# The merge of two branches: both halves in the same form, all their ways through DRAM on SyncE's queue

## The chip, the core and the metric

The kernel runs on one core of a Trainium2 chip. The metric is the time of one execution in microseconds (us) of device time, as the median of several runs. The profile is a hardware trace of one execution. Its engines are TensorE (PE; PEld is its weight load), VectorE (DVE), ScalarE (ACT), GpSimd (POOL) and SyncE (SP), which here only issues DMAs.

## The reference, cut to what matters

One decoder layer over 256 tokens of 1024 features, in float32: a feed-forward block, a mixing sub-layer with two branches, a second feed-forward block and a final norm. The change lies at the end of the mixing sub-layer:

```python
y_attn = attn @ w_branch_attn[l]       # (256, 512) @ (512, 1024)
y_gmlp = gm @ w_branch_gmlp[l]         # (256, 512) @ (512, 1024)
gates = jax.nn.sigmoid(n @ w_gate[l] + b_gate[l])
merged = gates[..., :D] * y_attn + gates[..., D:] * y_gmlp
h = h + merged @ w_out[l]
h = h + 0.5 * swiglu(rmsnorm(h, ffn2_norm[l]), ffn2_w_gate[l], ffn2_w_up[l], ffn2_w_down[l])
```

## The kernel before, in words

**Precision.** Every float32 operand of a product is split into a high and a low part (`split`, L192): ACT casts the source to the high part (L193), DVE subtracts it to get the low part (L195). A product is then three matmuls, high by high, high by low and low by high (`mm3`, L186 to L190). The output projection works the other way around, with weights stationary (`by_passes`, L169): per block of 128 input features one matmul of 512 columns (L162) takes high and low activations side by side, and one of 256 (L167) the low weights.

**Weights.** They come in units of two half units of 512 KB. `fetch_to` (L129) issues the fetches on SyncE (L137) into seven raw buffers, `split_half` (L139) splits them into a ring of four split units, and `unit(i, ahead)` (L154) hands out unit i after splitting up to i + ahead: 3 ahead for `ALONE`, 2 for `PAIRED`. A raw buffer is free again when its half unit has been subtracted on DVE, a place in the ring when the matmuls of the unit four earlier are done. The four units of the branch products are numbered from `mb` (gMLP, attention, gMLP, attention; 512 output columns each), then come four of the projection (`mo`) and those of the second feed-forward (`f2`).

**Order.** TensorE and SyncE run in the order in which the program is written. In this part DVE and ACT do so too (`in_order`, L208). A DMA issue on ACT therefore stands in line with ACT's casts, and a fetch on SyncE in line with the other transfers there.

**The merge (L704 to L763).** Tokens are in partitions: for token halves j = 0, 1 the branch products come in PSUM, DVE multiplies by the gates (in `gates`, the attention's in the first 1024 columns, the gMLP's in the second), adds the two, and transposes 32 x 32 squares (L720). The projection needs features in partitions. The squares are put in place by a **way** through DRAM: a write-out to `m_way` (`leave`, L723) and four fetch-backs into `m_back`, one for each 32 partitions (`from_way`, L358 to L363). `settle` (L725) then splits what came back, 128 features at a time, into `mT` (in the profile `mg`).

The 1024 columns go in three pieces: 0 to 255, 256 to 511 and 512 to 1023. In the first two, the gMLP's and the attention's products for one token half share one PSUM bank and one multiplication (L743) gates both. The write-out is on ACT's queue, the fetch-backs on SyncE's. In the third, the products are 512 columns wide, each with its own multiplication (L754); after each branch one of the first two pieces is settled (L758). Its write-out goes per token half on ACT, and its eight fetch-backs (L760) are on ACT too.

The projection (`down_features`, L252, called at L767) has eight accumulators in the eight PSUM banks (a pool in which banks are taken in turn) and goes through the four units: unit 0 and 1 need piece 0 and piece 1, units 2 and 3 the third. Unit 0 is computed for six accumulators first, then for the last two. `unit` is called at the head of each; `behind` runs after the first and the second unit, and there `third` (L762) settles the third piece. After the last unit come the residual, the norm's high and low parts, and the second feed-forward (L768 on).

Of the kernel before, what the change touches and what calls it, by code (L numbers as in the profile page):

```python
# [18 lines left out]
P = 128  # L19
# [26 lines left out]
def block_kernel(ctx, tc, t, out):  # L46
# [107 lines left out]
    def unit(i, ahead=PAIRED):  # L154
        split_to(i + 1 + ahead)
        return parts[i]
# [29 lines left out]
    def mm3(ps, st, mv_, first, last):  # L186
        (sh, sl), (mh, ml) = st, mv_
        nc.tensor.matmul(ps, sh, mh, start=first, stop=False)  # L188
        nc.tensor.matmul(ps, sh, ml, start=False, stop=False)  # L189
        nc.tensor.matmul(ps, sl, mh, start=False, stop=last)  # L190
# [164 lines left out]
                    mm3(ps[j], st, (w[:, k, 0, :], w[:, k, 1, :]), u + k == 0, u == 1 and k == 3)  # L355
        return ps

    def from_way(to, way, queue=nc.sync, js=slice(NT)):  # L358

        squares32 = way.rearrange("(q r) a n -> r q a n", r=32)  # L360
        qs = slice(4 * js.start if js.start else 0, 4 * js.stop)
        for a in range(4):
            queue.dma_start(to[32 * a:32 * a + 32, qs], squares32[:, qs, a, :])  # L363

    def by_token(way):
        return way.rearrange("(j p) a n -> p j (a n)", p=P)
# [6 lines left out]
    class Hidden:  # L373
# [22 lines left out]
        def leave(self, c):  # L396
            p, e = divmod(c, 2)
            n = 32 * self.blocks(p)
            if e == 0:
                self.way[p] = dram.tile([S, 4, n], F32, name=f"{self.name}way{p}")  # L400
            nc.sync.dma_start(by_token(self.way[p])[:, :, CH * e:CH * (e + 1)], self.turned.pop(c))
# [110 lines left out]
    with in_order():  # L512
# [178 lines left out]
        for j in range(NT):  # L691
# [9 lines left out]
        gate(3, chunk(mg, nT2, "g", 3))  # L701


        pieces = ((0, 256), (256, 256), (512, 512))  # L704
        m_way = [dram.tile([S, 4, n // 4], F32, name=f"mway{c0}") for c0, n in pieces]
        m_turned = [tmp.tile([P, NT, n], F32, tag="hg", name=f"mt{c0}") for c0, n in pieces[:2]] + [ut]
        m_back = [mix_b[:, b:b + n // S * 2].rearrange("p a (q n) -> p (a q) n", n=n // 4)
                  for b, (c0, n) in zip((8, 10, 12), pieces)]

        def branch(ps, i, of, j, c0, n):  # L710
            w, c = unit(mb + i, ALONE if i != 1 else PAIRED), c0 % 512
            for k in range(4):
                st = tuple(p[:, j * P:(j + 1) * P] for p in block_of([of], k))
                mm3(ps, st, tuple(w[:, k, two, c:c + n] for two in range(2)), k == 0, k == 3)

        def merged(p, j):
            c0, n = pieces[p]
            m = gates[:, j, c0:c0 + n]
            nc.vector.tensor_add(m, m, gates[:, j, D + c0:D + c0 + n])
            nc.vector.transpose(m_turned[p][:, j], m)  # L720

        def leave(p, js=slice(NT)):
            nc.scalar.dma_start(by_token(m_way[p])[:, js], m_turned[p][:, js])  # L723

        def settle(p):  # L725
            c0, n = pieces[p]
            for b in range(n // P):
                k = c0 // P + b
                settle_in(mT[k // 4][:, k % 4:k % 4 + 1], m_back[p][:, :, b * 32:(b + 1) * 32])

        aoT, = alloc_T("ao", ("nC",))
        for hp in range(4):
            attend(hp)
        both = ((1, gmT), (0, aoT))
        for p in range(2):
            c0, n = pieces[p]
            pbs = [bank(f"pb{p}{j}") for j in range(NT)]
            for q, j in [(q, j) for q in range(2) for j in range(NT)] if p == 0 else [(q, j) for j in range(NT) for q in range(2)]:
                at, of = both[q]
                branch(pbs[j][:, at * n:(at + 1) * n], q, of, j, c0, n)  # L740
                if q:
                    m = gates[:, j].rearrange("p (q c) -> p q c", q=2)[:, :, c0:c0 + n]
                    nc.vector.tensor_mul(m, pbs[j].rearrange("p (q c) -> p q c", q=2), m)  # L743
                    merged(p, j)
            leave(p)
            from_way(m_back[p], m_way[p])
        mT = alloc_T("mg", ("nA", "nB"))
        c0, n = pieces[2]
        for q, (at, of) in enumerate(both):
            for j in range(NT):  # L750
                ps = bank(f"pb2{q}{j}")
                branch(ps, 2 + q, of, j, c0, n)
                m = gates[:, j, at * D + c0:at * D + c0 + n]
                nc.vector.tensor_mul(m, ps, m)  # L754
                if q:
                    merged(2, j)
                    leave(2, slice(j, j + 1))
            settle(q)  # L758
        for j in range(NT):
            from_way(m_back[2], m_way[2], nc.scalar, slice(j, j + 1))  # L760

        def third():  # L762
            settle(2)  # L763


        nT3 = alloc_T("n3", ("nC", "nD"))
        down_features(mo, 4, lambda k: both_of(mT, k), 1.0, gain3, nT3, "3", "aT", 1, [lambda: None, third])  # L767
        hidden = Hidden("f2")  # L768
        sums = [chunk(f2, nT3, "f2", 0), chunk(f2, nT3, "f2", 1, [0])]
        rs = token_factors("3")  # L770
# [70 lines left out]
def _packed(inputs):  # L841
# [12 lines left out]
    def columns(g, n):  # L854
# [8 lines left out]
             for n in (1, 2)}  # L863
# [5 lines left out]


    four = np.arange(512).reshape(4, 4, P // 4).transpose(1, 0, 2).reshape(-1)
    merged = np.concatenate([c0 + np.arange(256).reshape(4, 2, P // 4).transpose(1, 0, 2).reshape(-1)
                             for c0 in (0, 256)] + [512 + four])

    def chunks(w):
        return w.reshape(2, 4, P, -1, 512).transpose(3, 0, 2, 1, 4).reshape(-1, P, 4, 512)
# [38 lines left out]
```

## Time and profile before

| | |
|---|---|
| median of 3 runs | 534.79 us (534.17 to 535.75) |
| profiled execution, its own time | 533.75 us |
| its span in the trace | 532.0 us |
| mean granted clock of TensorE | 0.993 |
| busy: PE, PEld, DVE, ACT | 518.8, 435.2, 356.9, 264.5 us |
| DMA | 124.72 MB, 234 GB/s on average |

Instructions are named by the line that issued them, often a helper's; `out<-in` gives the tiles written and read. A releaser is what ended an engine's idle time. Stretches are in microseconds from the start of the span. A granted clock of 1.00 is 2.4 GHz, and 1.2 GHz is half of it; a mean between them mixes both.

### The profile page before, as it was taken

What the parts mean: (1) busy time and instruction counts of PE and PEld (TensorE: products, weight loads), DVE (VectorE), ACT (ScalarE), POOL (GpSimd) and SP (SyncE); (2) the same over time, 40 slices, a digit from 0 to 9 for tenths busy, and PEclk for the clock granted to TensorE, in tenths of its full rate; (3) what the DMA queues carried; (4) which work ended last, traced back from release to release, by engine and by line L of the source; (5) the groups of instructions that cost most, each with busy time, mean ns of one, the idle gap of its engine ahead of it and who ended that gap; (6) DMA issues with size and microseconds to landing.
All of it is one profiled execution on the core that took longest, in us unless ns stands there. A gap on an engine that the chain in (4) does not pass through costs nothing.

```text
span 532.0 us, 6846 instructions
## 1 busy us (share of the span) xinstructions
PE 518.8 (98%) x2490; PEld 435.2 (82%) x2490; DVE 356.9 (67%) x493; ACT 264.5 (50%) x366; POOL 12.2 (2%) x20
## 2 busy tenths in 40 slices
PE   9999999999999999999999996999999999999995
PEld 7888888888888888888888985888888888888884
DVE  6886676665454689489876683789764765575424
ACT  7754454544354466659555243467443544463402
POOL 0010000000000001000000000001000000000002
PEclk9999999999999999999999999899999999999998
DMA  8999597979677239977899375629798779677302
GB/s 320 368 338 308 163 340 257 273 206 279 187 199 282 80 123 337 346 217 205 247 326 356 124 205 170 235 80 321 238 250 297 229 276 334 177 240 230 137 0 79
DMA packets 60657, 124.72 MB, mean 234 GB/s; under 512 B 9424, under 2 KB 34000, under 8 KB 60496
## 3 DMA queue, kind: packets, MB, share of 16 engines
q1 hardware_dynamic: 58352, 122.39, 71.5%
q10 hardware_dynamic: 2272, 1.90, 1.1%
q8 instruction: 19, 0.31, 0.2%
q14 instruction: 14, 0.11, 0.1%
HBM read 112.21 MB, written 12.06 MB: 234 GB/s over the span
## 4 chain that ended last, share of the span: by engine, by line
PE 84%; DMA 6%; DVE 4%; issue 2%; ACT 1%; SPq 0%; ACTq 0%; POOLq 0%; DVEq 0%; POOL 0%
PE f L188 14%; PE f L189 14%; PE f L190 14%; PE acc L162 9%; PE acc L167 5%; PE acch L190 4%; PE acch L188 4%; PE acch L189 4%; PE g L190 3%; PE g L189 3%; PE g L188 3%; DVE w L195 2%; DMA qk<-qkway 2%; DMA qback<-qkway 1%; DMA qkway<-mixed 1%
## 5 line engine op out<-in xcount | busy, mean ns | idle before, releaser
L195 DVE TENSOR_TENSOR w<-raw,w 128x1024 fp32r<-128x1024 f32 x180 | 211.7, 1217 | 84.4 <-ACT w L193 84.1
L193 ACT CAST w<-raw 128x1024 fp32r<-128x1024 f32 x180 | 179.6, 1048 | 104.3 <-PE f L190 47.3
L190 PE MATMUL f<-w,n 128*128 128x512 f32 x336 | 130.7, 389 | 0.0
L188 PE MATMUL f<-w,n 128*128 128x512 f32 x336 | 130.7, 389 | 0.0
L189 PE MATMUL f<-w,n 128*128 128x512 f32 x336 | 130.7, 389 | 0.0
L190 PEld LDWEIGHTS f<-w,n 128*128 128x128 f32 x336 | 63.1, 188 | 13.2
L188 PEld LDWEIGHTS f<-w,n 128*128 128x128 f32 x336 | 63.1, 188 | 13.1
L189 PEld LDWEIGHTS f<-w,n 128*128 128x128 f32 x336 | 63.1, 188 | 13.0
L162 PE MATMUL acc<-f1h,w 128*128 128x512 f32 x176 | 43.4, 391 | 0.0
L162 PEld LDWEIGHTS acc<-f1h,w 128*128 128x128 f32 x176 | 31.9, 188 | 5.8
L188 PE MATMUL acch<-w,f2h 128*128 128x512 f32 x84 | 32.7, 389 | 0.0
L190 PE MATMUL acch<-w,f2h 128*128 128x512 f32 x84 | 32.7, 389 | 0.0
L189 PE MATMUL acch<-w,f2h 128*128 128x512 f32 x84 | 32.7, 389 | 0.0
L388 ACT ACTIVATE f2s<-f,rstd 128x256 f32<-128x256 f32 x22 | 10.3, 474 | 30.2 <-PE f L190 28.9
L188 PE MATMUL g<-w,n 128*128 128x512 f32 x64 | 24.9, 389 | 0.0
L189 PE MATMUL g<-w,n 128*128 128x512 f32 x64 | 24.9, 389 | 0.0
L190 PE MATMUL g<-w,n 128*128 128x512 f32 x64 | 24.9, 389 | 0.0
L167 PEld LDWEIGHTS acc<-f1h,w 128*128 128x128 f32 x176 | 23.5, 191 | 1.5
L162 PE MATMUL acc<-mg,w 128*128 128x512 f32 x64 | 18.6, 424 | 5.6 <-DVE mg L195 5.6
L167 PE MATMUL acc<-f1h,w 128*128 128x256 f32 x176 | 23.9, 282 | 0.0
L390 DVE SCALAR_TENSOR_TENSOR f2a<-f,rstd,f2s 128x256 f32<-128x256 f32 x22 | 10.5, 476 | 19.4 <-ACT f2s L388 19.4
L388 ACT ACTIVATE f1s<-f,rstd 128x256 f32<-128x256 f32 x22 | 10.3, 473 | 24.3 <-PE f L190 22.8
(173 smaller groups left out, 623.7 us busy)
## 6 DMA issues: line engine op xcount, KB each, us to landing
raw<-in_f SPq DMA_DIRECT2D x84, 512.0 KB, 6.5
raw<-in_f1d SPq DMA_DIRECT2D x22, 512.0 KB, 6.2
raw<-in_f2d SPq DMA_DIRECT2D x22, 512.0 KB, 6.0
raw<-in_gate SPq DMA_DIRECT2D x16, 512.0 KB, 6.9
raw<-in_out SPq DMA_DIRECT2D x8, 512.0 KB, 5.6
f1way<-f1t SPq DMA_DIRECT2D x11, 256.0 KB, 6.4
f2way<-f2t SPq DMA_DIRECT2D x11, 256.0 KB, 5.5
front<-in_first SPq DMA_DIRECT2D x7, 384.0 KB, 5.8
```

The lines of the kernel that those rows point to most:

```text
L162: nc.tensor.matmul(ps, st, both.rearrange("p two n -> p (two n)"), start=first, stop=last)
L167: nc.tensor.matmul(ps[:, n:], st, both[:, 0, :], start=False, stop=False)
L188: nc.tensor.matmul(ps, sh, mh, start=first, stop=False)
L189: nc.tensor.matmul(ps, sh, ml, start=False, stop=False)
L190: nc.tensor.matmul(ps, sl, mh, start=False, stop=last)
L193: nc.scalar.copy(hi, src)
L195: nc.vector.tensor_sub(lo, src, hi.bitcast(F32))
L388: nc.scalar.activation(sg, ps[j][:, :CH], AF.Silu, scale=rs[j])
L390: nc.vector.scalar_tensor_tensor(a, ps[j][:, CH:], rs[j], sg, op0=ALU.mult, op1=ALU.mult)
```

## The change

Both halves of the 1024 columns are handled by one function, `merge(hf)`. First the gMLP's products of 512 columns are computed and gated for both token halves, then the attention's in two quarters of 256 columns. Each quarter is multiplied, added, transposed and written out at once, and after both write-outs of a half come its eight fetch-backs. All write-outs and fetch-backs are on SyncE's queue, and ACT issues none. In the second half a quarter of the first is settled after each gMLP product. The attention's unit of the first half is asked for with `ALONE`, that of the second with `PAIRED`, so that one unit of projection weights is split at each `unit` call of the merge except the last, and the third unit of the projection at the head of its first. `behind` settles quarter 2 after the projection's first unit and quarter 3 after its second. On the host, the order of the projection's input features follows the quarters. The other calls of `from_way` do the same as before.

```diff
-    def from_way(to, way, queue=nc.sync, js=slice(NT)):
+    def from_way(to, way):
...
-            queue.dma_start(to[32 * a:32 * a + 32, qs], squares32[:, qs, a, :])
+            nc.sync.dma_start(to[32 * a:32 * a + 32], squares32[:, :, a, :])
...
-        pieces = ((0, 256), (256, 256), (512, 512))
-        m_way = [dram.tile([S, 4, n // 4], F32, name=f"mway{c0}") for c0, n in pieces]
...
+        m_way = [dram.tile([S, 4, UC // 4], F32, name=f"mway{p}") for p in range(4)]
+        m_turned = {}
+        m_back = [mix_b[:, b:b + 2].rearrange("p a (q n) -> p (a q) n", n=UC // 4) for b in (8, 10, 12, 14)]
...
+        def merge(hf):
+            w = unit(mb + 2 * hf, ALONE)
+            for j in range(NT):
+                ps = bank(f"pg{hf}{j}")
+                branch(ps, w, gmT, j, slice(512))
+                m = gates[:, j, D + 512 * hf:D + 512 * (hf + 1)]
+                nc.vector.tensor_mul(m, ps, m)
+                if hf:
+                    settle(j)
+            w = unit(mb + 2 * hf + 1, PAIRED if hf else ALONE)
+            for p in (2 * hf, 2 * hf + 1):
+                m_turned[p] = tmp.tile([P, NT, UC], F32, tag="hg", name=f"mt{p}")
+                for j in range(NT):
+                    ps = bank(f"pa{p}{j}")[:, :UC]
+                    branch(ps, w, aoT, j, slice((p % 2) * UC, (p % 2 + 1) * UC))
+                    m = gates[:, j, p * UC:(p + 1) * UC]
+                    nc.vector.tensor_mul(m, ps, m)
+                    nc.vector.tensor_add(m, m, gates[:, j, D + p * UC:D + (p + 1) * UC])
+                    nc.vector.transpose(m_turned[p][:, j], m)
+                nc.sync.dma_start(by_token(m_way[p]), m_turned[p])
+            for p in (2 * hf, 2 * hf + 1):
+                from_way(m_back[p], m_way[p])
...
-        for p in range(2):
...
-                    nc.vector.tensor_mul(m, pbs[j].rearrange("p (q c) -> p q c", q=2), m)
-                    merged(p, j)
-            leave(p)
-            from_way(m_back[p], m_way[p])
+        merge(0)
         mT = alloc_T("mg", ("nA", "nB"))
...
-                if q:
-                    merged(2, j)
-                    leave(2, slice(j, j + 1))
-            settle(q)
-        for j in range(NT):
-            from_way(m_back[2], m_way[2], nc.scalar, slice(j, j + 1))
...
+        merge(1)
...
-        down_features(mo, 4, lambda k: both_of(mT, k), 1.0, gain3, nT3, "3", "aT", 1, [lambda: None, third])
+        down_features(mo, 4, lambda k: both_of(mT, k), 1.0, gain3, nT3, "3", "aT", 1,
+                      [lambda: settle(2), lambda: settle(3)])
```

## Rows read from the trace of the kernel before

**Rows 1.** TensorE's waits, whole execution: line, what it waited for, us in all, times, longest.

```profile
PE acc L162 <- DVE mg L195: 5.6, 2, 4.5
```

**Rows 2.** The table by stretches: length, busy us (x instructions) of each engine, granted clock, DMA.

```profile
293.32:304.94 11.62, 11.62 (x99) 11.62 (x98) 8.14 (x15) 2.48 (x5) 0.00 (x0) 1.00 0.35 122
304.94:315.84 10.90, 10.90 (x50) 9.01 (x49) 9.03 (x12) 6.41 (x8) 0.00 (x0) 1.00 0.59 145
315.84:332.94 17.10, 11.52 (x66) 9.84 (x64) 8.80 (x14) 4.54 (x9) 0.00 (x0) 1.00 0.62 206
332.94:340.19 7.25, 7.25 (x33) 6.16 (x33) 5.49 (x7) 3.17 (x4) 0.00 (x0) 0.76 0.86 280
340.19:345.78 5.59, 5.59 (x35) 4.88 (x33) 4.54 (x12) 2.65 (x6) 0.00 (x0) 1.00 0.47 185
345.78:525.00 179.22, 179.22 (x801) 148.76 (x800) 114.08 (x156) 83.28 (x104) 3.96 (x5) 1.00 0.65 209
```

**Rows 3.** Timeline of TensorE: start, us, instruction, in brackets the idle time before it.

```profile
315.84 2.88 PE L162 MATMUL acc<-mg,w 128*128 128x512 f32 x12
...
322.67 3.90 PE L162 MATMUL acc<-mg,w 128*128 128x512 f32 x16 [1.11 <-DVE mg L195]
...
332.94 5.50 PE L162 MATMUL acc<-mg,w 128*128 128x512 f32 x16 [4.46 <-DVE mg L195]
```

**Rows 4.** Timeline of ACT, the same stretch (ACTq: a DMA issue).

```profile
319.25 2.39 ACTq L723 DMA_DIRECT2D mway<-mixed  x2
321.75 0.71 ACT L193 CAST mg<-mixed 128x256 fp32r<-128x256 f32 x2 [8.05 <-DMA raw<-in_f]
322.46 6.55 ACTq L363 DMA_DIRECT2D mixed<-mway  x8
329.11 1.99 ACT L193 CAST w<-raw 128x1024 fp32r<-128x1024 f32 x2 [6.65 <-DMA mixed<-mway]
331.01 1.32 ACT L193 CAST mg<-mixed 128x256 fp32r<-128x256 f32 x4
```

**Rows 5.** Timeline of DVE, the same stretch.

```profile
322.19 0.76 DVE L195 TENSOR_TENSOR mg<-mixed,mg 128x256 fp32r<-128x256 f32 x2 [0.93 <-ACT mg L193]
330.19 2.36 DVE L195 TENSOR_TENSOR w<-raw,w 128x1024 fp32r<-128x1024 f32 x2 [7.24 <-ACT w L193]
332.46 1.43 DVE L195 TENSOR_TENSOR mg<-mixed,mg 128x256 fp32r<-128x256 f32 x4
```

**Rows 6.** Groups of DVE's instructions from 290 to 346, by form: busy us, mean ns.

```profile
L754 DVE TENSOR_TENSOR mixed<-pb,mixed 128x512 f32<-128x512 f32 x4 | 2.6, 674 | 0.0
L720 DVE STREAM_TRANSPOSE mt<-mixed 128x256 f32<-128x256 f32 x4 | 1.8, 445 | 0.1
...
L195 DVE TENSOR_TENSOR ao<-po,ao 128x256 fp32r<-128x256 f32 x4 | 1.4, 418 | 1.0 <-ACT ao L193 1.0
```

**Rows 7.** DMA issues, whole execution: transfer, queue, count, KB each, median us to landing.

```profile
raw<-in_f SPq DMA_DIRECT2D x84, 512.0 KB, 6.5
...
gmback<-gmway SPq DMA_DIRECT2D x4, 128.0 KB, 10.4
mway<-mt ACTq DMA_DIRECT2D x2, 256.0 KB, 2.8
mixed<-mway SPq DMA_DIRECT2D x8, 64.0 KB, 2.1
...
mixed<-mway ACTq DMA_DIRECT2D x8, 64.0 KB, 4.5
```

**Rows 8.** The way's DMA issues: ns min/median/max of one issue, first and last start.

```profile
L363 SPq DMA_DIRECT2D mixed<-mway x8: 302/445/612, 304.5 to 310.6; - x8
```

**Rows 9.** SyncE's own waits from 311 to 324.

```profile
SPq L137 <- DMA mway<-mixed: 6.1, 1, 6.1
```

**Rows 10.** DMA queue of SyncE from 304.5 to 306.9: packets, MB, share of 16 engines.

```profile
q1 hardware_dynamic: 730, 0.18, 32.1%
```

**Rows 11.** DMA queue of ACT from 322 to 330, the same columns.

```profile
q10 hardware_dynamic: 1276, 0.78, 36.0%
```

More of the change, by code (lines that the diff above doesn't have):

```diff
@@ L356, in chunk @@
         return ps
-    def from_way(to, way, queue=nc.sync, js=slice(NT)):
+    def from_way(to, way):
         squares32 = way.rearrange("(q r) a n -> r q a n", r=32)
-        qs = slice(4 * js.start if js.start else 0, 4 * js.stop)
         for a in range(4):
-            queue.dma_start(to[32 * a:32 * a + 32, qs], squares32[:, qs, a, :])
+            nc.sync.dma_start(to[32 * a:32 * a + 32], squares32[:, :, a, :])
     def by_token(way):
@@ L701, in block_kernel @@
         gate(3, chunk(mg, nT2, "g", 3))
-        pieces = ((0, 256), (256, 256), (512, 512))
-        m_way = [dram.tile([S, 4, n // 4], F32, name=f"mway{c0}") for c0, n in pieces]
[L706 to L711, printed above, removed]
+        m_way = [dram.tile([S, 4, UC // 4], F32, name=f"mway{p}") for p in range(4)]
@@ L712, in branch @@
+        m_turned = {}
+        m_back = [mix_b[:, b:b + 2].rearrange("p a (q n) -> p (a q) n", n=UC // 4) for b in (8, 10, 12, 14)]
+        def branch(ps, w, of, j, c):
             for k in range(4):
                 st = tuple(p[:, j * P:(j + 1) * P] for p in block_of([of], k))
[L714 to L720, printed above, removed]
@@ L722, in leave @@
-        def leave(p, js=slice(NT)):
-            nc.scalar.dma_start(by_token(m_way[p])[:, js], m_turned[p][:, js])
+                mm3(ps, st, tuple(w[:, k, two, c] for two in range(2)), k == 0, k == 3)
         def settle(p):
-            c0, n = pieces[p]
-            for b in range(n // P):
-                k = c0 // P + b
+            for b in range(2):
+                k = 2 * p + b
                 settle_in(mT[k // 4][:, k % 4:k % 4 + 1], m_back[p][:, :, b * 32:(b + 1) * 32])
+        def merge(hf):
[20 more added lines that the diff above has]
+                from_way(m_back[p], m_way[p])
@@ L733, in block_kernel @@
             attend(hp)
-        both = ((1, gmT), (0, aoT))
-        for p in range(2):
[L736 to L740, printed above, removed]
-                if q:
-                    m = gates[:, j].rearrange("p (q c) -> p q c", q=2)[:, :, c0:c0 + n]
-                    nc.vector.tensor_mul(m, pbs[j].rearrange("p (q c) -> p q c", q=2), m)
-                    merged(p, j)
-            leave(p)
-            from_way(m_back[p], m_way[p])
-        mT = alloc_T("mg", ("nA", "nB"))
-        c0, n = pieces[2]
-        for q, (at, of) in enumerate(both):
-            for j in range(NT):
[L751 to L755, printed above, removed]
-                    merged(2, j)
-                    leave(2, slice(j, j + 1))
-            settle(q)
-        for j in range(NT):
-            from_way(m_back[2], m_way[2], nc.scalar, slice(j, j + 1))
-        def third():
-            settle(2)
+        merge(0)
+        mT = alloc_T("mg", ("nA", "nB"))
+        merge(1)
         nT3 = alloc_T("n3", ("nC", "nD"))
-        down_features(mo, 4, lambda k: both_of(mT, k), 1.0, gain3, nT3, "3", "aT", 1, [lambda: None, third])
+        down_features(mo, 4, lambda k: both_of(mT, k), 1.0, gain3, nT3, "3", "aT", 1,
+                      [lambda: settle(2), lambda: settle(3)])
         hidden = Hidden("f2")
@@ L871, in _packed @@
     four = np.arange(512).reshape(4, 4, P // 4).transpose(1, 0, 2).reshape(-1)
-    merged = np.concatenate([c0 + np.arange(256).reshape(4, 2, P // 4).transpose(1, 0, 2).reshape(-1)
-                             for c0 in (0, 256)] + [512 + four])
+    merged = np.concatenate([p * UC + np.arange(UC).reshape(4, 2, P // 4).transpose(1, 0, 2).reshape(-1)
+                             for p in range(4)])
     def chunks(w):
```

## The prediction

> **What bounds the kernel now.** I read the list of TensorE's waits first. Over the whole execution it has one entry of size: the output projection's matmuls (L162) waited twice for DVE to finish `mg`, the merged activations in two parts, 5.6 us in all, the longer time 4.5 [rows 1]. Next the table by stretches [rows 2]. The branch products take 11.62 and 10.90 us with TensorE busy throughout; from the second feed-forward's first matmul at 345.78 to 525.00 it is busy 179.22 of 179.22 us. Only the projection between them has holes: 17.10 us with 11.52 busy, then 7.25 and 5.59 us for its third and fourth unit. Both are 32 matmuls, 16 of 512 columns and 16 of 256. The fourth ran at a granted clock of 1.00 (2.4 GHz) and is the price of a unit: 5.59 us (matmuls 0.227 us apart at 512 columns, 48 in 10.90 us). The third ran at a mean of 0.76, partly at 1.2 GHz, right after the longer wait, and cost 1.66 more. Four units at 5.59 are 22.36 us; the stage from 315.84 to 345.78 took 29.94. **7.58 us are lost here**, and since TensorE is the bound from 345.78 on, what is won here should reach the end.
>
> Which wait ends last is read from the timelines. The last pieces of `mg` come from the third way (columns 512 to 1023). ACT issues its two write-outs up to 321.64, so the casts of the second piece, next in ACT's program, begin only at 321.75; that is TensorE's first hole, up to 322.67 [rows 3, 4]. Then ACT issues eight fetch-backs, 6.55 us with their waits, until 329.01. Behind them in program order stand two casts of the projection's last weight unit (329.11), and only then the casts of the third piece (331.01) [rows 4]. DVE mirrors this: two weight subtractions of 2.36 us from 330.19, `mg` from 332.46 [rows 5]. TensorE's second hole ends at 332.94 [rows 3]. So the chain is ACT as a DMA issuer, then a weight split that stands ahead of the piece TensorE wants.
>
> **The change, part by part.** *Products.* Before, eight groups of 12 matmuls are 256 columns wide and four are 512; afterwards it is the same eight and four in another order. TensorE's products therefore still end at 315.84: nothing gained or lost. The half stages are 5.45 us (gMLP, half of 10.90) and 5.81 (attention, half of 11.62), so they end at 298.77, 304.58, 310.03 and 315.84 [rows 2].
>
> *DVE before the first ways.* Its multiplications are separate now: for each quarter and token half a product from PSUM (0.418, as the like operation on `ao`), an addition (the same price) and a transpose (0.445), together 1.28 us [rows 6]. The 512-column products cost 0.67 each. A unit of projection weights is now split between the gMLP and the attention products of each half, ahead of these on DVE. The first split can't start before the gMLP matmuls free its buffer, a little after 298.77; I take 299.2. The first subtraction follows 1.08 us after the cast (329.11 to 330.19 in the rows), the pair takes 2.36, and it ends at 302.6 [rows 4, 5]. Quarters 0 and 1 then leave at 305.2 and 307.7. DVE's second split lasts to 310.1, the first product after it to 310.8.
>
> *A way's length.* A write-out lands 2.8 us after issue, four fetch-backs are issued 0.44 us apart, and the last lands 2.1 later: 6.25 us [rows 7, 8]. Quarter 0 is back at 311.5 and quarter 1 at 314.0. Settling one (two casts 0.71, two subtractions 0.76, overlapping [rows 4, 5]) takes 1.15, so the first two quarters of `mg` are ready at 312.6 and 315.1. This is where the change **adds a wait**: on DVE, the settling of quarter 1 stands in front of the products of quarters 2 and 3, which TensorE had ready from 311.5 on. Quarter 2's second product is read from PSUM at 316.8; quarters 2 and 3 leave at 317.7 and 320.2. Who waits for that: the eight PSUM banks are taken in turn, so the projection's sixth accumulator needs the bank of that product, and TensorE wants it at 315.84 + 5 × 0.227 = 316.98. The margin is 0.2 us, less than my steps are sure of; I take a stall of 0.2. The seventh and eighth are wanted at 320.0 or later, and free at 318.1 and 319.4.
>
> *The second half's ways.* All on SyncE, in order: write-out 2, write-out 3 (320.2), then fetch-backs 2 from 320.7. They land at 324.1, and settling ends at 325.3. TensorE, after the stall and two units, wants this at 315.84 + 0.2 + 11.18 = 327.2: **covered, by 1.9 us**. Quarter 3 is written by 323.1, back at 326.5, and settled behind the last weight split at about 329.1, wanted at 332.8. The weight split that stood ahead of the third piece still stands ahead of the last quarter, but a unit of matmuls now covers it.
>
> *ACT and SyncE.* ACT loses all 12 DMA issues; what it waits for is then the data. SyncE gets them: 20 way transfers where it had 8. The two fetches ahead of write-out 0 wait for the split that ends at 302.6, so they don't hold it. What is queued behind the ways are the fetches of the second feed-forward's first weights. The fourth and fifth half units now leave behind the last fetch-back, at about 325. Such a fetch was held before too, 6.1 us by a way's write-out whose data it doesn't use [rows 9]. Landing 6.5 us after issue [rows 7] they are there at about 331.8, and TensorE needs those weights at 338.4. Cost nothing; without this cover each late microsecond would be paid.
>
> *Short rows.* In the second half the rows that a fetch-back reads shrink from 512 to 256 bytes. Between 304.5 and 306.9, while quarter 0 came back, the queue moved 730 packets of about 250 bytes in 32.1% of 16 engines' 2.4 us: 17 ns each [rows 10]. In the 8 us of ACT's fetch-backs 1276 packets of 611 bytes on average took 36.0%: 36 ns [rows 11]. Per byte that is nearly alike, so I add nothing. If a short packet instead held an engine for twice those 36 ns, a quarter's 1024 packets would take 3.5 us longer on 16 engines, 1.6 of it uncovered (1.9 are covered, above), and the sum below would be -5.8 in place of -7.4. The Trainium skill ("DMA: Bandwidth & Descriptors", Specifications) speaks for that outcome and against the change: it puts line rate at 512 bytes and more, with a read-modify-write below. By that page I would write -5.8, by the row -7.4; the 17 ns disagree with the page.
>
> *Sum.* The projection takes 22.36 + 0.2 instead of 29.94: **-7.4 us**. The profiled execution took 533.75 (its span of 532.0 and 1.75 around it), so 526.35; it lies 1.04 under the median of the runs, 534.79, and the forecast for the median is 527.4.
>
> **Bounds.** The unknown is how long the ways take on SyncE beside weight fetches. If each took x us longer, TensorE would stall x at the sixth accumulator, and x - 1.9 more before the third unit, since two ways follow each other. Nearest row: SyncE's own fetch-backs, x = 0, which I take since the same queue issued the same sizes. ACT's landed after 4.5 us [rows 7]: x = 2.4, 2.9 us in all, 530.3. Below nothing: the 0.2 could vanish, and the fastest run shown is 0.6 under the median: 526.5. More can't be won in this stage.
>
> **The rivals.** *Half kept:* the ways land as ACT's did, and a new stall at the accumulators takes part of the gain: 530.3. For it: the margin of 0.2 us. Against it: SyncE's rows. *Short rows* at 72 ns a packet: 3.5 us longer in the second half, 1.6 of it paid: 529.0; against it stand the 17 ns measured on the same form. *Nothing at the end:* the later fetches of second feed-forward weights make TensorE wait for these, and the 7.4 us are given back: 534.8. For it: two half units leave only at about 325. Against it: 6 us from landing to use. *Slower:* the place is DVE's queue, where settling quarters 0 and 1 now blocks products that are ready. A fetch-back of the same kind earlier in the kernel, `gmback`, landed after 10.4 us among weight fetches [rows 7]. At x = 8.3 the stalls are 2 × 8.3 - 1.9 = 14.7 us, against 7.4 won: 542.1. It decides from x = 4.65, a landing after 6.75 us. Against it: SyncE's program has only two weight fetches just ahead of these ways and two between the halves. *The change doesn't do what it says* if the eight issues were slow from the transfers and not from ACT's place; that is the first rival's case.
>
> **How the numbers follow.** Forecast 0.70, half kept 0.16, short rows 0.02, nothing 0.05, slower 0.07. About 0.3% (1.6 us) can be told from no change. The first three are faster: 0.88; same 0.05; slower 0.07. The range runs from 526.4 to 531.0, which takes in the forecast, the bounds and the first two rivals (0.88 before the run-to-run spread).
>
> **What would show it.** Right: TensorE's waits without the two for `mg`; a granted clock of 1.00 through the projection; its first matmul still near 315.8 and the feed-forward's first at about 338.4; no DMA issues on ACT before the end; write-outs 2 and 3 near 317.7 and 320.2; the third unit's start near 327.2. Wrong: a wait of TensorE for DVE's product of quarter 2 or 3 within the first unit, fetch-backs that land after more than 4 us, a wait before the third unit, or, after 338, TensorE waiting for weight subtractions. A feed-forward that starts 7 us earlier with the end not moved would refute the claim that TensorE bounds the rest.

## The result and the profile after

The changed kernel takes **527.03 us** (median of 6 runs, 526.43 to 530.29) against 534.81 for the kernel before (6 runs, 533.04 to 535.75). The ratio is 0.9864, 95% interval 0.9837 to 0.9892. That is 7.8 us less by the medians and 7.3 by the ratio, where 7.4 had been forecast. A second series of six, further down, has 528.17 us and a ratio of 0.9888 [0.9865, 0.9912], 6.0 us less. Two disturbed executions, of 1061.56 us (the kernel before) and 2986.19 us (its version with the ways on SyncE), are left out of the medians and ratios below.

The profiled execution is the longest of the six, 530.29 us, span 528.6. Its merge begins late, for a reason far upstream (the wait for `qk`, taken up at the end); so times are compared with before after adding 3.82, the difference between the first branch products, 297.14 against 293.32. TensorE's waits, as [rows 1]:

```profile
PE sc L552 <- DMA qk<-qkway: 2.2, 2, 1.7
PE warm L94 <- DVE zeros L91: 1.2, 1, 1.2
```

Both waits for `mg` are gone. What is left of the stage is a stall too short for that list; it stands among the waits of TensorE's weight loads:

```profile
PEld acc L162 <- DVE mixed L734: 0.3, 1, 0.3
```

The table by stretches (length, busy us of PE, PEld, DVE, ACT and POOL, granted clock, DMA share, GB/s), cut as [rows 2]: the branch products, the projection's four units, and the rest.

```profile
297.16:319.69 22.53, 22.53 (x146) 20.61 (x146) 17.30 (x32) 8.78 (x15) 0.00 (x0) 1.00 0.55 174
319.69:325.47 5.78, 5.78 (x34) 4.83 (x33) 5.54 (x13) 1.01 (x2) 0.00 (x0) 1.00 0.35 126
325.47:331.06 5.59, 5.59 (x35) 4.92 (x33) 2.44 (x4) 2.30 (x4) 0.00 (x0) 1.00 0.53 131
331.06:336.63 5.57, 5.57 (x35) 4.92 (x34) 5.26 (x7) 4.82 (x7) 0.00 (x0) 1.00 0.86 293
336.63:342.22 5.59, 5.59 (x35) 4.88 (x34) 5.45 (x12) 2.05 (x4) 0.00 (x0) 1.00 1.01 381
342.22:521.50 179.28, 179.28 (x801) 148.86 (x800) 114.52 (x158) 83.97 (x106) 3.96 (x5) 1.00 0.66 212
```

Every unit of the projection now costs what only the fourth cost before, at a granted clock of 1.00. From the first branch product to the feed-forward's first matmul, which is called **the stage** below, it is 342.22 - 297.14 = 45.08 us against 345.78 - 293.32 = 52.46: 7.38 less. The rest is as long as before, 179.28 us, and without a hole.

SyncE's timeline shows where the ways went (four write-outs, and their fetch-backs between the weight fetches):

```profile
308.95 2.88 SPq L737 DMA_DIRECT2D mway<-mt  x2
312.47 3.78 SPq L362 DMA_DIRECT2D mixed<-mway  x8
316.35 0.87 SPq L137 DMA_DIRECT2D raw<-in_f  x2
321.83 2.88 SPq L737 DMA_DIRECT2D mway<-mt  x2
325.12 3.82 SPq L362 DMA_DIRECT2D mixed<-mway  x8
```

And ACT's, the casts that settle quarters 0, 1 and 2, in place of [rows 4]:

```profile
316.23 0.71 ACT L193 CAST mg<-mixed 128x256 fp32r<-128x256 f32 x2 [5.53 <-DMA mixed<-mway]
318.09 0.71 ACT L193 CAST mg<-mixed 128x256 fp32r<-128x256 f32 x2 [1.14 <-DMA mixed<-mway]
...
328.76 0.71 ACT L193 CAST mg<-mixed 128x256 fp32r<-128x256 f32 x2 [8.06 <-DMA mixed<-mway]
```

ACT waits for the data alone, and each piece is there before TensorE wants it: quarter 2 is subtracted on DVE from 329.20 to 329.96, the third unit begins at 331.06. DVE's second product of quarter 2, which frees the sixth accumulator's bank, and that subtraction:

```profile
320.48 0.39 DVE L734 TENSOR_TENSOR mixed<-pa,mixed 128x256 f32<-128x256 f32 x1
...
329.20 0.76 DVE L195 TENSOR_TENSOR mg<-mixed,mg 128x256 fp32r<-128x256 f32 x2 [2.65 <-ACT mg L193]
```

The landing times, as [rows 7]:

```profile
mway<-mt SPq DMA_DIRECT2D x4, 256.0 KB, 2.3
mixed<-mway SPq DMA_DIRECT2D x16, 64.0 KB, 2.2
```

### The profile page after: what moved, and what is told of

Same layout as the page of the kernel before. It is cut to its first block, busy times and chain, and to the rows that moved or that the text cites. A ratio compares the mean times of both kernels' runs of the same rounds, so it can differ in the third digit from the quotient of the medians.

```text
span 528.6 us, 6857 instructions
## 1 busy us (share of the span) xinstructions
PE 518.8 (98%) x2490; PEld 435.1 (82%) x2490; DVE 357.3 (68%) x501; ACT 265.1 (50%) x366; POOL 12.2 (2%) x20
## 4 chain that ended last, share of the span: by engine, by line
PE 89%; DMA 5%; DVE 3%; issue 1%; ACT 1%; SPq 0%; POOLq 0%; DVEq 0%; POOL 0%; ACTq 0%
PE f L190 14%; PE f L188 14%; PE f L189 14%; PE acc L162 10%; PE acc L167 5%; PE acch L190 4%; PE acch L189 4%; PE acch L188 4%; PE g L188 3%; PE g L190 3%; PE g L189 3%; DVE w L195 2%; DMA qkway<-mixed 2%; DMA qk<-qkway 2%; DMA qback<-qkway 2%
## 5 line engine op out<-in xcount | busy, mean ns | idle before, releaser
L188 PEld LDWEIGHTS acch<-w,f2h 128*128 128x128 f32 x84 | 15.8, 188 | 3.3
```

## The experiments

The change does several things at once: it moves the ways to SyncE's queue, moves a weight split (`PAIRED` for the second half's attention unit), cuts the last piece into quarters and reorders the products. The prediction blamed two things for the second hole: ACT as issuer, and a weight split ahead of the piece. Undone or done alone they give (us; stage from the first branch product to the feed-forward's first matmul, in the profiled execution; "hole" is TensorE's idle time before the third unit). The stage is the sharper measure: the totals also spread by what happens upstream. The changed kernel's two traces have 45.08 and 45.36, so 0.3 us of stage say nothing:

| kernel | median (range, runs) | ratio to before [95%] | stage | hole |
|---|---|---|---|---|
| before | 534.81 (533.04 to 535.75, 6) | 1 | 52.46 | 4.46 |
| changed | 527.03 (526.43 to 530.29, 6) | 0.9864 [0.9837, 0.9892] | 45.08 | 0 |
| before, ways on SyncE | 533.29 (532.20 to 534.97, 9) | 0.9975 [0.9952, 0.9999] | 52.36 | 4.51 |
| before, `PAIRED` | 533.56 (531.98 to 534.53, 10) | 0.9975 [0.9961, 0.9988] | 51.87 | 4.37 |
| before, both of these | 529.97 (528.56 to 532.50, 5) | 0.9904 [0.9870, 0.9937] | 49.15 | 2.46 |
| changed, 2nd half on ACT | 529.25 (527.50 to 534.43, 10) | 0.9887 [0.9850, 0.9923] | 47.42 | 1.51 |
| changed, last settling later | 526.37 (526.18 to 531.27, 4) | 0.9854 [0.9795, 0.9913] | 45.34 | 0 |
| changed, fetch-backs cut in two | 532.80 (531.10 to 537.80, 10) | 0.9976 [0.9940, 1.0012] | 51.31 | 0 |
| changed, `ALONE` | 532.96 (531.18 to 534.96, 10) | 0.9948 [0.9925, 0.9970] | 51.35 | 0 |
| changed, 2nd half in one | 530.52 (527.07 to 533.51, 10) | 0.9921 [0.9888, 0.9954] | 46.76 | 1.96 |
| changed, again | 528.17 (526.50 to 531.54, 6) | 0.9888 [0.9865, 0.9912] | 45.36 | 0 |
| changed, settling between | 526.72 (525.86 to 528.46, 4) | 0.9859 [0.9839, 0.9878] | 44.86 | 0 |
| the same, keys first | 526.03 (525.66 to 526.21, 5) | 0.9841 [0.9829, 0.9854] | 44.87 | 0 |

The kernel before had medians of 534.78, 535.35 and 534.64 beside them. A gain "by the ratio" is one minus the ratio, times the median of the kernel before that was taken beside it; its 95% interval stands behind it. The stage of the ways on SyncE comes from another execution than the nine of its line.

### The kernel before with its ways on SyncE's queue

```diff
         def leave(p, js=slice(NT)):
-            nc.scalar.dma_start(by_token(m_way[p])[:, js], m_turned[p][:, js])
+            nc.sync.dma_start(by_token(m_way[p])[:, js], m_turned[p][:, js])
...
-            from_way(m_back[2], m_way[2], nc.scalar, slice(j, j + 1))
+            from_way(m_back[2], m_way[2], nc.sync, slice(j, j + 1))
```

> The kernel before, with its write-outs and the third piece's fetch-backs moved from ACT's queue to SyncE's and nothing else. The stage is measured from the first branch product to the second feed-forward's first matmul: 52.46 us before, 45.08 after. Theory (ACT's hold as a DMA issuer made both holes): settling of the second piece no longer waits on ACT, the casts of the last weight unit come early, the third piece is back at about 327; holes of 0.5 and 0.3 us stay, no half clock; stage about 45.7, total about 528.1. Rival (the quarters and the moved weight splits pay, the queue does little): only the first hole goes, stage about 51, total about 533.5.

Measured 533.29: the rival's total. The queue alone is worth 1.3 us by the ratio (0.1 to 2.6). A second measurement of the same kernel has a trace of the stage.

> The kernel before with all the merge's ways on SyncE once more, to see where the expected 6.7 us stay: it gained 1.3 us. Theory A: the last-but-one projection unit is still split, and two weight fetches still issued, ahead of the third piece's write-outs, so these leave no earlier than before, and the fetch-backs share the queue with the two fetches; a hole of 4 us or more stays before the third unit, with half clock after it, and the way's landings are well over 2.2 us. Theory B: the landings are 2 to 2.5 us and another wait took the hole's place.

One run, 534.61, stage 52.36, as theory A has it: of the 7.4 us that the whole change takes from the stage, the queue alone takes 0.1, which can't be told from nothing. SyncE's timeline, its DMA issues, and TensorE's second hole with the third unit's stretch:

```profile
313.06 3.66 SPq L137 DMA_DIRECT2D raw<-in_f  x5
...
318.46 2.38 SPq L723 DMA_DIRECT2D mway<-mixed  x2
...
325.69 4.41 SPq L363 DMA_DIRECT2D mixed<-mway  x8
```

```profile
mway<-mixed SPq DMA_DIRECT2D x2, 256.0 KB, 6.4
```

```profile
332.60 6.68 PE L162 MATMUL acc<-mg,w 128*128 128x512 f32 x16 [4.51 <-DVE mg L195]
```

```profile
332.60:341.03 8.43, 8.43 (x32) 7.05 (x33) 5.58 (x7) 4.19 (x6) 0.00 (x0) 0.65 0.74 243
```

The first hole has gone: ACT no longer issues ahead of the second piece's casts. What that gave is lost again behind the second: the third unit costs 8.43 us at a granted clock of 0.65, where it cost 7.25 at 0.76 [rows 2]. The second hole is as long as before, with another cause. The two write-outs stand on SyncE's queue behind six weight fetches of 512 KB (one `raw<-in_out` at 312.56 and the five shown; one of the six had landed when the first write-out was issued), and land after 6.4 us (median). On ACT's queue, in the kernel before, they landed after 2.6 us (median). SyncE's queue from 314 to 324 (packets, MB, share of 16 engines), here and then in the kernel before:

```profile
q1 hardware_dynamic: 947, 3.28, 97.6%
```

```profile
q1 hardware_dynamic: 654, 2.35, 71.1%
```

The DMA engines had next to no time free here; before, a fetch was held back by a write-out [rows 9]. Whether the order on one queue or the fetches themselves made the write-outs late is taken up in the last section. The first fetch-back leaves at 325.69 instead of 322.46 [rows 4]. Now ACT waits for nothing but the data:

```profile
316.99 2.15 ACT L193 CAST w<-raw 128x1024 fp32r<-128x1024 f32 x2 [1.89 <-PE pb L190]
331.68 1.32 ACT L193 CAST mg<-mixed 128x256 fp32r<-128x256 f32 x4 [12.54 <-DMA mixed<-mway]
```

The weight cast that stood behind the fetch-backs in [rows 4] is done from 316.99 on, far ahead, and nothing is won by it.

### The kernel before with only the weight split moved

```diff
-            w, c = unit(mb + i, ALONE if i != 1 else PAIRED), c0 % 512
+            w, c = unit(mb + i, ALONE if i % 2 == 0 else PAIRED), c0 % 512
```

> The kernel before with PAIRED in place of ALONE for the last attention unit and nothing else; the write-outs and the third piece's fetch-backs stay on ACT. Theory (the two parts need each other): the products are gated 2 us earlier, but the fetch-backs hold ACT, and now two units' casts instead of one stand behind them and ahead of the third piece; a hole of about 4 us and half clock stay; stage 50 to 52.5 (52.5 before), total 532.5 to 535. Rival (the place of the split is the whole gain): stage 46 or less, total under 529.

Measured 533.56, stage 51.87, as the theory has it: 0.6 us of the stage, 1.3 by the ratio (0.6 to 2.1). ACT's timeline shows a gain that is given back, and TensorE's the hole:

```profile
316.75 2.39 ACTq L723 DMA_DIRECT2D mway<-mixed  x2
...
321.36 3.72 ACTq L363 DMA_DIRECT2D mixed<-mway  x8
325.17 3.89 ACT L193 CAST w<-raw 128x1024 fp32r<-128x1024 f32 x4 [5.15 <-DMA mixed<-mway]
328.96 1.32 ACT L193 CAST mg<-mixed 128x256 fp32r<-128x256 f32 x4
```

```profile
331.27 6.34 PE L162 MATMUL acc<-mg,w 128*128 128x512 f32 x16 [4.37 <-DVE mg L195]
```

Without a split between the products (2.35 us on DVE) the write-outs leave 2.5 us earlier (319.25 in [rows 4]), and the eight fetch-backs are issued by 325.08 instead of 329.01. But the split that was moved now stands with its neighbour behind ACT's issues and ahead of the third piece: four casts instead of two, and on DVE 4.63 us instead of 2.36. The first hole is gone; the second ends when the third piece has been subtracted behind that split, and stays 4.37.

### Both together

> The kernel before with all the merge's ways on SyncE, and PAIRED in place of ALONE for the last attention unit, as in the changed kernel: the split of the projection's third unit and the two fetches that go with it move behind the third piece's ways. Theory A: the third piece's products are gated 2 us earlier, its ways have the queue to themselves, and both holes all but close; total 527.5 to 528.5, like the changed kernel. Rival (the quarters and the separate gMLP products are needed): 531 or more.

Measured 529.97, stage 49.15, between the two expectations: 3.3 us of the stage (5.1 by the ratio, 3.4 to 7.0), more than the 0.1 and 0.6 of the parts. Each removes what kept the other from paying: on SyncE's queue ACT is free for the moved split while the way is under way (DVE does it from 318.26 to 322.88), and with the split moved the write-outs leave earlier. What is left of the hole (SyncE, DVE's four weight subtractions, the write-outs' landing, TensorE):

```profile
311.49 1.33 SPq L137 DMA_DIRECT2D raw<-in_f  x3
315.01 3.04 SPq L723 DMA_DIRECT2D mway<-mixed  x2
...
321.27 5.21 SPq L363 DMA_DIRECT2D mixed<-mway  x8
```

```profile
318.26 4.62 DVE L195 TENSOR_TENSOR w<-raw,w 128x1024 fp32r<-128x1024 f32 x4
```

```profile
mway<-mixed SPq DMA_DIRECT2D x2, 256.0 KB, 5.2
```

```profile
329.10 5.53 PE L162 MATMUL acc<-mg,w 128*128 128x512 f32 x16 [2.46 <-DVE mg L195]
```

The write-outs still follow weight fetches (the three shown and one `raw<-in_out`, none of them landed at 315.01) and land after 5.2 us (median). The changed kernel has two fetches behind the first ways, both landed before the second write-outs are issued, and those land after 2.1 and 2.5. The 4.1 us between this stage and the changed kernel's 45.08 were taken apart only as far as the quarters of the second half, below.

### The changed kernel with the second half's ways on ACT

```diff
...
-                nc.sync.dma_start(by_token(m_way[p]), m_turned[p])
+                (nc.scalar if hf else nc.sync).dma_start(by_token(m_way[p]), m_turned[p])
...
-                from_way(m_back[p], m_way[p])
+                from_way(m_back[p], m_way[p], nc.scalar if hf else nc.sync)
```

> The changed kernel with the second half's two write-outs and eight fetch-backs on ACT's queue. Theory: ACT is held by them from the second write-out on, so the casts of the third projection unit start only behind the last fetch-back, about 8 us later than in the changed kernel; a hole of about 1.7 us before the third unit, none elsewhere; stage about 46.8, total about 528.8. Rival 1 (the queue alone is all of the gain): the holes come back whole, stage about 52, total about 534.5. Rival 2 (the queue is worth nothing, order and quarters are): no change, stage 45.1, total 527.

Measured 529.25, stage 47.42, as the theory has it. ACT's timeline and TensorE's third unit:

```profile
322.54 2.87 ACTq L737 DMA_DIRECT2D mway<-mt  x2
325.45 4.04 ACTq L362 DMA_DIRECT2D mixed<-mway  x8
329.59 2.00 ACT L193 CAST w<-raw 128x1024 fp32r<-128x1024 f32 x2 [10.09 <-DMA mixed<-mway]
331.49 0.71 ACT L193 CAST mg<-mixed 128x256 fp32r<-128x256 f32 x2
```

```profile
333.42 3.92 PE L162 MATMUL acc<-mg,w 128*128 128x512 f32 x16 [1.51 <-DVE mg L195]
```

The pattern of before returns, fetch-backs, then the split, then the piece, but it costs 1.51 us and not 4.46: these eight issues take 4.04 us and land after 2.2, where those of before took 6.55 and 4.5. No weight fetch was under way beside them. In the kernel before, one was issued on SyncE at 322.50 and landed at 327.38; ACT's first fetch-back, of 322.46, landed at 327.59, and ACT, which had issued six by 325.26, issued the seventh at 327.61. So the queue is worth about 2.3 us of the stage once the rest of the change is there.

### A split ahead of the piece, with ACT free

```diff
-                      [lambda: settle(2), lambda: settle(3)])
+                      [lambda: None, lambda: (settle(2), settle(3))])
```

> The changed kernel with quarters 2 and 3 both settled after the projection's second unit, so that the last weight split stands ahead of quarter 2 again, as it stood ahead of the third piece before. Theory of the prediction's first part (a split in front is paid): 2.0 us of casts and 2.4 of subtractions come in front, and past the 1.1 us of slack that the trace after shows, a hole of about 1 to 1.3 before the third unit; total about 528.2. Rival (the split stood there only because ACT reached it late; free of DMA issues, ACT does it while the way is still under way): stage 45.1, total unchanged at 527.

Measured 526.37, stage 45.34: the rival, no cost that can be told from the changed kernel's 45.08 and 45.36. (The median of four runs, one of them 531.27, says less.) With no issues in its program ACT does all four weight casts from 314.63 on, long before quarter 2 lands, and settles it at 324.68:

```profile
314.63 3.90 ACT L193 CAST w<-raw 128x1024 fp32r<-128x1024 f32 x4
324.68 0.71 ACT L193 CAST mg<-mixed 128x256 fp32r<-128x256 f32 x2 [6.16 <-DMA mixed<-mway]
```

A weight split ahead of the wanted piece costs only where something holds it back.

### Longer issues

```diff
...
         for a in range(4):
-            nc.sync.dma_start(to[32 * a:32 * a + 32], squares32[:, :, a, :])
+            for qs in cuts:
+                nc.sync.dma_start(to[32 * a:32 * a + 32, qs], squares32[:, qs, a, :])
```

with `cuts` of two halves in the merge, so 16 issues a half stage in place of eight.

> The changed kernel with each of the merge's fetch-backs cut in two halves of the tokens: 32 issues of 32 KB in place of 16 of 64 KB. It lengthens the ways by SyncE's issue time: quarter 1 and quarter 3 by about 3.4 us, quarters 0 and 2 by 1.8. Theory (DVE's settling in front of ready products, then the accumulators): a stall of about 3.6 us before the sixth accumulator in place of 0.2, and about 0.7 before the third unit; stage about 49.2, total about 531. Rival (the matmuls cover the ways, DVE's order costs nothing): under 1 us, total under 528.

Measured 532.80, stage 51.31: 6.2 us of stage, and a total that can't be told from the kernel before. The sixteen issues take 7.47 us against 3.78, the settling of quarter 1 is 4.0 us later, and the products behind it on DVE keep the accumulators' banks:

```profile
320.27 0.80 PE L162 MATMUL acc<-mg,w 128*128 128x512 f32 x1 [2.77 <-DVE mixed L735]
321.52 3.36 PE L162 MATMUL acc<-mg,w 128*128 128x512 f32 x7 [0.45 <-DVE mixed L735]
```

Seven matmuls took 3.36 us where the same seven took 1.88 with the second half on ACT, after a stall of 0.49: half the clock after the longer stall. From 321.00 to 326.00 the granted clock was 0.50. Of the 6.2 us, 3.0 are the longer stalls, and the other 3.2 go with the clock; neither expectation had these.

### The changed kernel with `ALONE` in the second half

```diff
-            w = unit(mb + 2 * hf + 1, PAIRED if hf else ALONE)
+            w = unit(mb + 2 * hf + 1, ALONE)
```

> The changed kernel with ALONE in place of PAIRED for the last attention unit: the split of the projection's third unit stands ahead of the products of quarters 2 and 3 on DVE, and two weight fetches ahead of their write-outs on SyncE. Theory A: 2.3 us of subtractions delay the products of quarter 2; a stall of about 2.6 us before the fifth and sixth accumulator, some half clock after it, and later ways; total 530 to 532. Rival (the place of the split doesn't matter while the queue is SyncE's): 527.

Measured 532.96, stage 51.35, beyond theory A: one word is worth 6.3 us of the stage. DVE, then TensorE:

```profile
315.99 2.36 DVE L195 TENSOR_TENSOR w<-raw,w 128x1024 fp32r<-128x1024 f32 x2 [0.50 <-ACT w L193]
```

```profile
318.74 0.50 PE L162 MATMUL acc<-mg,w 128*128 128x512 f32 x1 [2.49 <-DVE mixed L734]
319.99 3.36 PE L162 MATMUL acc<-mg,w 128*128 128x512 f32 x7 [0.74 <-DVE mixed L734]
```

The split of 2.36 us and the wait for its casts put quarter 2's products on DVE 3.6 us later. The accumulator stall grows from 0.2 to 3.2 us, and the half clock follows again (0.50 from 321.00 to 326.00): 3.2 us more. The two fetches that moved with the split cost nothing that shows; there is no hole before the third unit. The margin of 0.2 us was real.

### The second half in one piece

```diff
...
+            if hf:
+                for j in range(NT):
+                    ps = bank(f"paw{j}")
+                    branch(ps, w, aoT, j, slice(512))
...
+                nc.sync.dma_start(by_token(w_way), ut)
+                from_way(w_back, w_way)
+                return
...
```

> The changed kernel with the second half's attention products 512 columns wide, one write-out and four fetch-backs with rows of 512 bytes in place of the two quarters. Theory A: the way leaves at about quarter 3's time less 0.8 us and is back 0.8 us after quarter 2's time, inside the slack; the accumulators' banks are free earlier, as two products hold two banks and not four; total 526.5 to 527.2, so that the quarters of the second half buy nothing. Rival (the early first quarter is needed before the third unit): a hole of 1 us or more there, 528 or more.

Measured 530.52, stage 46.76: the rival. One write-out of 512 KB lands after 2.8 us, its four fetch-backs after 2.9, and the third unit waits 1.96 for the whole. The accumulator stall is gone. The second half's quarters are worth about 1.7 us of the stage: with them, the third unit's piece leaves 2.4 us earlier and arrives alone.

### The last stall, and the wait for the keys

The changed kernel was run again, and two versions of it. The first settles quarter 1 between the second half's quarters, behind the write-out of quarter 2:

```diff
-                if hf:
-                    settle(j)
+                if hf and j == 0:
+                    settle(0)
...
+                if p == 2:
+                    settle(1)
```

The second also issues the keys' four fetch-backs ahead of a chunk of gate weights, far upstream:

```diff
...
-        chunk(mgv, nT2, "gv", 0, [1], psgv)
         qk = act.tile([P, 2, 4 * S], F32, tag="nC", name="qk")
...
         from_way(kT, qk_way[1])
+        chunk(mgv, nT2, "gv", 0, [1], psgv)
```

> The changed kernel once more, beside the two versions below. Stage 45.1 as in its first profile; total 526.4 to 530.3 as before, with the spread from the queries' and keys' way upstream of the change: where that is late, the attention scores wait, and the profile's 3.9 us before the first branch product come back in some executions.

> The changed kernel with quarter 1 settled between quarter 2's and quarter 3's products in place of ahead of both. Theory: quarter 2's products no longer wait on DVE for quarter 1's way; the stall of 0.2 us at the sixth accumulator goes, and the write-out of quarter 2 leaves about 1.2 us earlier; the second unit, which needs quarter 1, still finds it 4 us early. Stage 44.9, total 0.2 us less than the changed kernel, which the timing can't tell. Rival: the later settling delays the second unit, stage 45.5 or more.

> As the one with quarter 1 settled between, and, well upstream, the fetch-backs of the keys issued ahead of two gate weight fetches in place of behind them. Theory: the keys are back about 4 us earlier, the attention scores don't wait for them in any execution (0.3 to 3.9 us before), the spread of the runs shrinks, and the median falls by 0.3 to 1.5 us against the changed kernel of this call. Rival: the fetches that now leave 5 us later make TensorE wait in the gate stage, and the median rises.

Measured 528.17 (one run, 531.54, lies above the range expected), 526.72 and 526.03; stages 45.36, 44.86 and 44.87, the last two as their theories have it. With the settling in between, the accumulators wait for nothing. The keys first take away TensorE's wait for `qk`; what TensorE's list still has is

```profile
PE warm L94 <- DVE zeros L91: 1.2, 1, 1.2
PE f L466 <- ACT n L442: 0.5, 1, 0.5
```

The runs now lie within 0.6 us (525.66 to 526.21), those of the changed kernel within 5.0. Each is one kernel with few runs, so the gain in the median over the changed kernel (2.1 us in the same series, 1.0 against 527.03) is less certain than the narrower range. The version with the keys first has the lowest median found here.

## Why the prediction was right, and where its reasons were not

**The sum** was right. The stage shrank by 7.38 us, forecast 7.4, and by 7.1 in the changed kernel's second trace. That the first median fell by 7.8 is as near as it is partly by luck: the second series has 6.0 by the ratio, and the runs of one kernel spread by several us. That TensorE bounds the rest is shown too: the feed-forward began 7.38 us earlier relative to the first branch product and the end followed.

**The products and DVE's queue.** Write-outs 0 and 1 were forecast at 305.2 and 307.7 and came at 308.95 and 311.5, which is 305.1 and 307.6 on the clock of before. Write-outs 2 and 3, forecast at 317.7 and 320.2, came at 318.0 and 320.5 (321.83 and 324.33 in the trace after). Quarter 2's second product left PSUM at 320.87, forecast 316.8 + 3.8 = 320.6, and the accumulators stalled 0.2 to 0.3 us as the step on the sixth accumulator had it. That this is the weak place was shown by delaying DVE there (`ALONE`, and longer issues): both brought the stall. One step was off and cost nothing: quarter 0 was forecast back at 311.5 and was back at 312.3 on the clock of before, since the first half's fetch-backs stand behind both write-outs on SyncE and waited for the first to land, after 3.5 us and not 2.8.

**The way's length** was right: write-outs after 2.1 to 3.5 us, fetch-backs after 2.0 to 2.5, but for the last two, of quarter 3, which took 3.8 and 3.5 and which only the fourth unit needs. Quarter 2 was ready at 329.96 where the forecast says 329.1 on this clock, so the slack before the third unit was 1.1 us and not 1.9.

**Short rows** cost nothing that shows in the stage, but not for the reason given. While quarters 0 and 1 came back, 1842 packets took 59.7% of 16 engines' 4.0 us, 21 ns each; while 2 and 3 did, 1849 packets took 61.1% of 4.0 us, also 21. [Rows 10] had 17. These are means over several sizes, and so were the prediction's 36 ns: that window held 1009 packets of 512 bytes and 128 of 2048, a whole write-out. Taken by size, the traces have a median of 18 ns for a packet of 256 bytes and 46 for 1024 (changed kernel), 27 for 512 (second half in one piece) and 159 for 4096 (weight fetches): 14, 22, 19 and 26 bytes per ns. So "nearly alike" per byte was too kind: rows of 256 bytes take a third more of the engines' time than rows of 512. For a quarter that is an estimated 0.3 us of 16 engines (1024 packets of 18 ns in place of 512 of 27), which the slack covers. The Trainium skill ("DMA: Bandwidth & Descriptors", Specifications) puts line rate at 512 bytes and more, with a read-modify-write below. The traces agree that shorter rows are slower by the byte; they show no jump at 512, where the rate is still 19 against 26, and nothing like the doubled packet of the prediction's rival. That is all in which "the 17 ns disagree with the page".

**Late weight fetches** cost nothing, as forecast: TensorE's lists have no wait after 342.22. The fetch behind the last fetch-back was issued at 329.03 and landed at 334.74, which is 325.2 and 330.9 on the clock of before, forecast 325 and 331.8.

**What failed is the first part's reading of the cause**, the sentence "So the chain is ACT as a DMA issuer, then a weight split that stands ahead of the piece TensorE wants." It describes the kernel before well, and the timeline with the split alone has both links again. But read as the cost it misleads. Taking ACT out as issuer won 0.1 us of the stage, since the write-outs then landed behind the weight fetches under way and the half clock, longer than before, took what the first hole gave; the split ahead of the piece cost nothing once ACT was free. The chain has a third link, the weight fetches under way beside the third piece's transfers, which wasn't in the list; only the end of the rivals doubts that ACT's eight issues were slow by ACT's place alone. That doubt was half right: of their 6.55 us, 2.35 passed between the sixth and the seventh, while a weight fetch was landing. The sum held because the prediction took its way lengths from SyncE's own rows and its write-out times from DVE's order, and the changed kernel's order gives both: no weight fetch is under way when the second half's write-outs and fetch-backs leave.

**The bound's formula**, "TensorE would stall x at the sixth accumulator, and x - 1.9 more before the third unit", is half confirmed. The stall at the accumulators came with the delay: quarter 2's products came 4.0 us later on DVE with the fetch-backs cut in two and 3.6 later with `ALONE`, and TensorE stalled 3.2 us in both. The second part did not come: TensorE, itself late, had no hole before the third unit. In its place came half the clock, 3.2 us, which no term had. At x of 4.0 and 3.6 the formula gives 6.1 and 5.3 us, and the stage lost 6.2 and 6.3: the size is near by luck, since the clock's loss is not the second stall.

## What to carry to other kernels

When a transfer is late, follow it to three places: the engine that issues it, the work that stands ahead of its data, and the large transfers under way beside it; taking away the first brought 0.1 us of the stage here, the second 0.6, both 3.3, and the whole order 7.4. Moving DMA issues to the queue of the weights frees the engine that issued them. It takes no weight fetch out of the way: order the program so that none is under way when the small urgent transfer leaves. A margin of 0.2 us is worth finding and testing: 2.4 us of work in the wrong place on DVE cost 6.3, because TensorE lost its clock too.

## What the runs showed that was not expected

- **A write-out lands behind the weight fetches under way, on whichever queue.** 256 KB landed after 2.1 to 2.5 us with no fetch under way (changed kernel, second half). In four kernels fetches were under way when the third piece's first write-out was issued, and it landed 0.67 to 0.69 us after the last of them: on ACT's queue 3.2 us after its issue (before) and 4.6 (split moved alone), on SyncE's 7.2 (queue alone) and 6.2 (both). The split alone and both together differ in the queue and nothing else, and the write-outs landed 28.3 and 28.9 us after the first branch product on ACT's queue, 28.4 and 29.1 on SyncE's, though on ACT's they had been issued 1.5 and 0.8 us later. While ACT's first write-out waited, from 316.7 to 318.9, SyncE's queue (q1) and ACT's (q10) moved (split alone; packets, MB, share of 16 engines):

```profile
q1 hardware_dynamic: 239, 0.86, 96.7%
q10 hardware_dynamic: 9, 0.02, 2.1%
```

  So the place on SyncE's queue doesn't explain the late write-outs, while the fetches under way go with them in all four. A kernel in which the fetches alone were moved was not run.
- **TensorE's clock after a hole.** After holes of 1.51 and 1.96 us the next 16 matmuls of 512 columns took 3.92 and 3.93 us, full speed; after 2.46, 4.37, 4.46 (before) and 4.51 us they took 5.53, 6.34, 5.50 and 6.68, part of it at half clock. The length of the hole alone does not decide it: after waits for `qk` of 1.3 and 0.9 us close together (second half on ACT) the granted clock fell, to a mean of 0.83 from 235 to 245; after waits of 1.5 and 0.7 there (settling between) it stayed at 1.00.
- **Part of the spread of the changed kernel's runs comes from elsewhere.** In the profiled execution the attention scores waited 2.2 us for the keys' fetch-backs, behind gate weights on SyncE's queue, and the granted clock fell:

```profile
225.00:235.00 10.00, 7.75 (x47) 6.30 (x47) 6.55 (x10) 4.32 (x5) 1.98 (x2) 0.98 1.00 244
235.00:245.00 10.00, 10.00 (x52) 8.26 (x51) 8.07 (x11) 6.68 (x18) 0.00 (x0) 0.85 0.41 123
```

With the fetch-backs issued first (the last version above) both stretches run at 1.00, with TensorE busy throughout, and the runs spread less. Nothing in the change touches this place, and why the wait varies from run to run was not tried.
